# Seven block products in place of eight in six places of a two-layer macaron trunk

## The chip, the core and the metric

The kernel runs on one core of a Trainium2 chip. The metric is the device time of one execution in microseconds, given as the median over runs. Its engines are named as in the profile: PE is TensorE (matmuls), PEld its weight loads, DVE is VectorE, ACT is ScalarE, POOL is GpSimd, SP is SyncE (which here issues the DMAs).

## The reference

The input is x with 256 rows of 1024, and the model has two layers. Each layer is a macaron: a feed-forward with weight one half, a mixer, and a second such feed-forward, each behind an RMSNorm. The mixer of layer 0 is a convolution module, that of layer 1 a latent attention. A last RMSNorm ends the trunk. The change touches the feed-forwards alone:

```python
def swiglu_ffn(h, w1, w3, w2):
    return (jax.nn.silu(h @ w1) * (h @ w3)) @ w2
...
    h = h + FFN_RES_WEIGHT * swiglu_ffn(rmsnorm(h, ffn_norm1[i]), ffn1_w1[i], ffn1_w3[i], ffn1_w2[i])
```

w1 and w3 are 1024 x 2816, w2 is 2816 x 1024, and everything is float32. There are four feed-forwards, called FFN 0 to FFN 3 here: FFN 0 and 1 lie around the convolution module, FFN 2 and 3 around the attention.

## The kernel before

**Numbers.** Every float32 operand is held as two parts, a high part in TensorE's rounded float32 and a low part, the difference. A product is three matmuls into one PSUM bank (`mm3`, L274): high by low, high by high, low by high.

**Weights.** All weights come as blocks of 128 x 2048 float32, 1 MB each, in the one order in which they are used (the list `blocks` in `trunk`, L85). `load` (L164) fetches a block on SP's queue into one of three raw buffers (`RAW_BUFS`); ScalarE casts it to the high part in two pieces of 128 x 1024 (L190), and VectorE subtracts for the low part in two pieces (L191). There are five pairs of high and low buffers (`W_BUFS`), so the cast of a block waits until the block five places earlier has been read by TensorE. `weights` (L216) hands out the next block and loads ahead of it.

**A feed-forward** (`ffn_in`, L705). The first product goes in five chunks of 512 columns of w1 and w3: four blocks, 96 matmuls and four PSUM banks a chunk. A sixth, half chunk (`both`) takes two blocks. After a chunk, for each of the two halves of 128 rows (`tb`), ScalarE takes the Silu (L805), VectorE multiplies (L806), and `turn` transposes the result: VectorE transposes within 32 x 32 squares (L352), four DMAs write it to DRAM (L356) and one reads it back (L360), ScalarE casts the high part Gh (L714) and VectorE subtracts for the low part Gl (L715). `first_chunk` (L717) is the order of chunk 0 where the rows come in late. The second product (`Rows`, L626) has 11 blocks of w2 of two k tiles each; `block` (L640) issues the 24 matmuls of a block into four banks (two halves of rows by two halves of columns), and `finish` (L647) does the last blocks, the addition to h and the start of the next norm.

**PSUM.** Tag A has four banks and serves the chunks and the second product's four sums in turn, tag B three, tag C one.

**What sets the order.** The program is written in the order above, and a list scheduler puts each engine's instructions in order by its own timeline and by what is due; `urgent` (L196) gives an operation precedence, `order` adds an order between two instructions without a wait. An engine works through its own instructions strictly in that order.

Of the kernel before, what the change touches and what calls it, by code (L numbers as in the profile page):

```python
# [11 lines left out]
F32 = mybir.dt.float32  # L12
F32R = mybir.dt.float32r
# [3 lines left out]
ALU = mybir.AluOpType  # L17
AX = mybir.AxisListType

P = 128  # L20
D = 1024
S = 256
NT = S // P
KT = D // P
# [60 lines left out]
def trunk(ctx: ExitStack, tc: tile.TileContext, x, xt, first, pos, invf, gfin, wdw,  # L85
# [14 lines left out]
    def uid(s):  # L100
        n_uid[0] += 1
        return f"{s}_{n_uid[0]}"
# [4 lines left out]
    def bank(tag, name):  # L107
        return ps.tile([P, 512], F32, tag=tag, name=uid(name), bufs=BANKS[tag])

    blocks = []
    conv_block = {}
    for i in range(2):
        for w13, w2 in ((f1w13, f1w2), (f2w13, f2w2)):

            for cc_ in range(5):
# [3 lines left out]
            blocks += [w2[i, a_] for a_ in range(NF // 2)]  # L121
# [36 lines left out]
    def raw_to(last):  # L158
        while len(loaded) + len(raws) < last:
            src = blocks[len(loaded) + len(raws)]  # L160
            raw = rawp.tile([P, HB], F32, tag="raw", name=uid("raw"))
            raws[len(loaded) + len(raws)] = raw, nc.sync.dma_start(raw[:, :src.shape[-1]], src)

    def load(src, pieces=1):  # L164
        if isinstance(src, tuple):
            raw = rawp.tile([P, HB], F32, tag="raw", name=uid("raw"))
            nc.sync.dma_start(raw, src[1])
            return raw
        n = src.shape[-1]
        there = len(loaded) in raws  # L170
        raw = raws.pop(len(loaded))[0] if there else rawp.tile([P, HB], F32, tag="raw", name=uid("raw"))
        hi = wp.tile([P, HB], F32R, tag="hi", name=uid("hi"))
        lo = wp.tile([P, HB], F32R, tag="lo", name=uid("lo"))
        if there:
            pass
        elif len(loaded) < 7:

            for i in range(pieces if len(loaded) < 4 else 1):
                c = slice(i * n // pieces, (i + 1) * n // pieces) if len(loaded) < 4 else slice(n)
                fetch(raw[:, c], src[:, c])  # L180
        else:
            dma = nc.sync.dma_start(raw[:, :n], src)
            if turns:

                order(dma, turns[-1].ins)
        for i in range(pieces):
            c = slice(i * n // pieces, (i + 1) * n // pieces)

            low = nc.gpsimd if len(loaded) == conv_block[-4] else nc.vector
            casts[len(loaded), i] = (nc.scalar.copy(hi[:, c], raw[:, c]),  # L190
                                     low.tensor_sub(lo[:, c], raw[:, c], hi[:, c].bitcast(F32)))  # L191
# [79 lines left out]

    keep_warm(WARM)

    def mm3(o, ah, al, bh, bl, start, stop, after=()):  # L274

        mm = nc.tensor.matmul(o, ah, bl, start=start, stop=False)  # L276
        for a in after:
            order(mm, a.ins)
        nc.tensor.matmul(o, ah, bh, start=False, stop=False)  # L279
        return nc.tensor.matmul(o, al, bh, start=False, stop=stop)  # L280

    def some(o, kinds, ah, al, bh, bl, start, stop):

# [342 lines left out]
    class Rows:  # L626
        def __init__(self, zh, zl, nk, last=False):
            self.zh, self.zl, self.nk, self.last = zh, zl, nk, last
            self.o = {(tb, d): bank("A", "o") for tb in range(NT) for d in range(2)}

        def mm(self, part, i, tb, d, o, f0, f1, o0=0, o1=512, after=(), after_last=()):
            hi, lo = part
            for j in range(2):
                f = 2 * i + j
                c = slice(j * D + d * 512 + o0, j * D + d * 512 + o1)
                mm = mm3(o, self.zh[:, f, tbs(tb)], self.zl[:, f, tbs(tb)], hi[:, c], lo[:, c], f == f0,
                         f == f1 - 1, [*after, *after_last] if j else after)
            return mm

        def block(self, i):  # L640
# [57 lines left out]
            return nxt  # L698


    def ffn(X, make_next, beside=lambda: None, apart=False):
        with tc.tile_pool(name=uid("ffn"), bufs=1) as act:
            return ffn_in(act, X, make_next, beside, apart)

    def ffn_in(act, X, make_next, beside, apart):  # L705
# [40 lines left out]
        for c in range(6):  # L746
# [4 lines left out]
            u = {}  # L751
            if c == 0 and X.pool:
                first_chunk(X, u)
            for m in range(0 if u else 1 if both else 2):
                parts = weights(KT // kn, c > 0 or m > 0)
                before = None
# [49 lines left out]
                nc.vector.tensor_mul(s[:, :w], s[:, :w], u[0, tb][:, w:] if both else u[1, tb])  # L806
                turn(c, tb, w, s)
        o = Rows(Gh, Gl, NF, make_next is Final)
        for i in range(NF // 2 - (3 if apart else 2)):
            o.block(i)  # L810
            beside()
        return o.finish(X.rh, make_next, act, apart)
# [743 lines left out]
def _layout(x, positions, ffn_norm1, ffn1_w1, ffn1_w3, ffn1_w2, mix_norm, ffn_norm2,  # L1556
# [18 lines left out]
    def rows(w):  # L1575

        k, n = w.shape
        return c(w.reshape(k // (2 * P), 2, P, n).transpose(0, 2, 1, 3)).reshape(k // (2 * P), P, 2 * n)

    def halves(w):  # L1580

        k, n = w.shape
        return c(w.reshape(2, k // (2 * P), P, n).transpose(0, 2, 1, 3)).reshape(2, P, -1)
# [11 lines left out]
    for k in range(KT):  # L1595
# [22 lines left out]
        "f1w2": np.stack([rows(ffn1_w2[i]) for i in range(2)]),  # L1618
        "f2w13": np.stack([up(ffn2_w1[i], ffn2_w3[i]) for i in range(2)]),
        "f2w2": np.stack([rows(ffn2_w2[i]) for i in range(2)]),  # L1620
        "cw1": np.concatenate(cw1),
        "cw2": rows(conv_w_pw2[0]),
        "wa": np.concatenate([waq, wak]),
# [26 lines left out]
```

## Time and profile before

| | |
|---|---|
| three runs | 917.29, 914.8 and 916.79 us, median 916.79 us |
| span of the profiled execution | 913.0 us |
| DMA over the span | 198.94 MB moved, 218 GB/s in the mean |
| DMA of raw blocks of w1 and w3, w2 (in_f2w) | 66 of 1024 KB, 5.0 us from issue to landing |
| the same for in_f1w | 62 of 1024 KB, 5.2 us |

The span is the time from the first to the last instruction that the profiler recorded in one execution; the runs are timed from outside and are some microseconds longer. A page of the profile gives the busy time of each engine and the chain of work that ended last, followed back from the end. A row of a group reads: line, engine, operation, what it writes and reads with shapes, how often, then the busy time in all with the mean of one in nanoseconds, then the idle time ahead of it and what ended most of that. A row of the timeline reads: start, duration, engine, line, operation, how often, and in brackets the idle time ahead of it. The operations of an engine overlap a little at their ends, so the distance between two starts is somewhat less than a duration.

### The profile page before, as it was taken

To read this page: it belongs to the slowest core of one execution; us is meant where nothing else is said; L and a number is where in the kernel's file an instruction comes from. 1 tells how busy PE (TensorE), PEld (TensorE's weight loads), DVE (VectorE), ACT (ScalarE), POOL (GpSimd) and SP (SyncE) were. 2 spreads that over 40 slices of the span, in tenths; PEclk is the share of its full clock that TensorE was granted. 3 is DMA by queue.
4 is the path that set the end of the run, shared out by engine and by line. 5 is a ranking of instruction groups with operands and counts; after the bars stand their busy time and mean duration, and the time that the engine had idled before them with its cause. 6 is when DMAs were issued, how large, how long until landed. Compare 5 with 4: busy or idle time off the path is not lost.

```text
span 913.0 us, 12107 instructions
## 1 busy us (share of the span) xinstructions
PE 905.5 (99%) x4305; PEld 761.7 (83%) x4305; DVE 596.1 (65%) x940; ACT 495.8 (54%) x845; POOL 129.2 (14%) x259
## 2 busy tenths in 40 slices
PE   9999999999999999999999999999999999999997
PEld 7888888898988888888888888888898888888886
DVE  6885764489997666664486665545768567566533
ACT  7654544388876544543375444433677565454432
POOL 1730000079951000000020000001400000000000
PEclk9999999999999999999999999999999999999999
DMA  9987776533237977775577677754635468767611
GB/s 336 323 286 262 265 265 221 193 139 139 94 105 239 319 242 260 248 243 212 186 281 253 247 246 238 230 212 133 219 139 185 143 238 311 246 218 278 226 47 47
DMA packets 71053, 198.94 MB, mean 218 GB/s; under 512 B 12368, under 2 KB 41936, under 8 KB 51664
## 3 DMA queue, kind: packets, MB, share of 16 engines
q1 hardware_dynamic: 70560, 197.47, 62.7%
q8 instruction: 34, 0.56, 0.2%
q10 hardware_dynamic: 432, 0.69, 0.2%
q14 instruction: 27, 0.22, 0.1%
HBM read 181.87 MB, written 16.25 MB: 217 GB/s over the span
## 4 chain that ended last, share of the span: by engine, by line
PE 99%; ACT 0%; POOL 0%; DVE 0%; issue 0%; ACTq 0%
PE u L280 17%; PE u L279 17%; PE u L276 17%; PE o L279 10%; PE o L276 10%; PE o L280 10%; PE u L844 3%; PE gate L844 3%; PE u L285 2%; PE o L1080 2%; PE tp L320 1%; PE pairs L887 1%; PE a L280 1%; PE a L276 1%; PE a L279 1%; PE nope L276 1%
## 5 line engine op out<-in xcount | busy, mean ns | idle before, releaser
L191 DVE TENSOR_TENSOR lo<-raw,hi 128x1024 fp32r<-128x1024 f32 (+1 forms) x292 | 344.6, 1219 | 164.1 <-ACT hi L190 157.8
L190 ACT CAST hi<-raw 128x1024 fp32r<-128x1024 f32 x294 | 292.6, 1045 | 222.4 <-PE o L280 76.9
L276 PE MATMUL u<-lo,Xh 128*128 128x512 f32 x672 | 261.7, 389 | 0.0
L280 PE MATMUL u<-hi,Xl 128*128 128x512 f32 x672 | 261.6, 389 | 0.0
L279 PE MATMUL u<-hi,Xh 128*128 128x512 f32 x672 | 261.5, 389 | 0.0
L276 PEld LDWEIGHTS u<-lo,Xh 128*128 128x128 f32 x672 | 126.1, 188 | 26.7 <-ACT Xh L471 0.3
L280 PEld LDWEIGHTS u<-hi,Xl 128*128 128x128 f32 x672 | 126.1, 188 | 26.4 <-DVE Xl L339 0.4
L279 PEld LDWEIGHTS u<-hi,Xh 128*128 128x128 f32 x672 | 126.1, 188 | 26.1
L279 PE MATMUL o<-hi,Gh 128*128 128x512 f32 (+1 forms) x356 | 137.7, 387 | 0.0
L280 PE MATMUL o<-hi,Gl 128*128 128x512 f32 (+1 forms) x356 | 137.7, 387 | 0.0
L276 PE MATMUL o<-lo,Gh 128*128 128x512 f32 (+1 forms) x356 | 137.1, 387 | 0.0
L311 POOL TENSOR_TENSOR ms<-ss 128x1 f32<-128x1 f32 x16 | 10.5, 661 | 580.0 <-ACT junk L303 580.0
L276 PEld LDWEIGHTS o<-lo,Gh 128*128 128x128 f32 x356 | 66.9, 188 | 13.7
L280 PEld LDWEIGHTS o<-hi,Gl 128*128 128x128 f32 x356 | 66.8, 188 | 13.6
L279 PEld LDWEIGHTS o<-hi,Gh 128*128 128x128 f32 x356 | 66.9, 188 | 13.5
L714 ACT CAST Gh<-gb 128x512 fp32r<-128x512 f32 (+1 forms) x48 | 28.0, 583 | 79.6 <-DMA gb<-gd 79.6
L715 DVE TENSOR_TENSOR Gl<-gb,Gh 128x512 fp32r<-128x512 f32 (+1 forms) x48 | 31.3, 652 | 58.8 <-ACT Gh L714 58.8
L933 DVE SCALAR_TENSOR_TENSOR acc<-V,dw,acc 128x128 f32<-128x128 f32 (+1 forms) x174 | 53.9, 392 | 0.0
L954 ACT ACTIVATE prod<-V,dw 128x128 f32<-128x128 f32 (+1 forms) x128 | 45.6, 415 | 1.8 <-POOL Y L955 1.0
L806 DVE TENSOR_TENSOR s<-s,u 128x512 f32<-128x512 f32 (+1 forms) x48 | 30.4, 634 | 5.7 <-PE u L280 5.5
L665 DVE SCALAR_TENSOR_TENSOR h<-o,rh,h 128x512 f32<-128x512 f32 (+1 forms) x18 | 12.9, 719 | 32.5 <-PE o L280 32.5
L805 ACT ACTIVATE s<-u,R 128x512 f32<-128x512 f32 (+1 forms) x48 | 31.1, 647 | 4.7 <-PE u L280 3.7
(225 smaller groups left out, 904.5 us busy)
## 6 DMA issues: line engine op xcount, KB each, us to landing
raw<-in_f2w SPq DMA_DIRECT2D x66, 1024.0 KB, 5.0
raw<-in_f1w SPq DMA_DIRECT2D x62, 1024.0 KB, 5.2
raw<-in_cw SPq DMA_DIRECT2D x12, 1024.0 KB, 4.8
gd<-gt SPq DMA_DIRECT2D x160, 64.0 KB, 3.4
gb<-gd SPq DMA_DIRECT2D x40, 256.0 KB, 4.6
raw<-in_wo SPq DMA_DIRECT2D x4, 1024.0 KB, 4.8
hd<-rows SPq DMA_DIRECT2D x56, 64.0 KB, 2.3
rows<-hd SPq DMA_DIRECT2D x14, 256.0 KB, 2.7
```

What stands on the lines that cost most here:

```text
L190: casts[len(loaded), i] = (nc.scalar.copy(hi[:, c], raw[:, c]), low.tensor_sub(lo[:, c], raw[:, c], hi[:, c].bitcast(F32)))
L191: low.tensor_sub(lo[:, c], raw[:, c], hi[:, c].bitcast(F32)))
L276: mm = nc.tensor.matmul(o, ah, bl, start=start, stop=False)
L279: nc.tensor.matmul(o, ah, bh, start=False, stop=False)
L280: return nc.tensor.matmul(o, al, bh, start=False, stop=stop)
L714: nc.scalar.copy(gh, bv)
L715: nc.vector.tensor_sub(Gl[:, f, tbs(tb)].rearrange("p t (i q) -> p t i q", q=32), bv, gh.bitcast(F32))
L805: nc.scalar.activation(s[:, :w], u[0, tb][:, :w], AF.Silu, scale=X.r[tb])
L806: nc.vector.tensor_mul(s[:, :w], s[:, :w], u[0, tb][:, w:] if both else u[1, tb])
L844: mm = nc.tensor.matmul(u[:, t], w[:, c], X.x[:, k, t], start=(k == 0), stop=(k == KT - 1))
L933: dve_last.append(nc.vector.scalar_tensor_tensor(out if j == j1 - 1 else y, v, w, y, op0=ALU.mult, op1=ALU.add))
L954: prods_last.append(nc.scalar.activation(p, v, AF.Copy, scale=w))
```

## The change

A product of two matrices cut into 2 x 2 blocks takes eight products of blocks. Strassen's method (here in Winograd's form) takes seven, whose operands are sums and differences of the blocks. In FFN 1, 2 and 3 it is used twice: for chunk 3 of the first product (2 x 2 blocks of the rows: two halves of k by two halves of rows; of the weights: two halves of k by w1 and w3), and for the first eight k tiles of the second product, the first four blocks of w2. That makes six places, each called a seven below. The host lays out the first eight k tiles of w2 so that a fetched block of 128 x 2048 is one of the 2 x 2 blocks.

- `load_seven` fetches the four blocks as before, one DMA each. It forms the operands of the weights with four VectorE subtractions of 128 x 2048 in the raw buffers, and makes high and low parts of seven operands instead of four.
- `forms_of` makes the four operands of the rows that are sums or differences: a GpSimd addition of 128 x 2048 (high and low part back to one number), four GpSimd additions or subtractions of 128 x 512, and for each of these a ScalarE cast and a VectorE subtraction. For the first product it is called ahead of chunk 2's products; for the second product it reads the turned results of chunks 0 and 1.
- `seven_products` issues seven products of four k tiles each, 84 matmuls in place of 96. Partial sums go from bank to bank: c21 is copied from c11 (ScalarE), `kept` is a copy of c22 (ScalarE), c12 is c21 + kept (VectorE) and c22 is c21 + kept (VectorE) at a later state of c21, and TensorE goes on adding into them.
- There are four raw buffers in place of three, and the builder is given a smaller scratch area for dynamic DMAs.

FFN 0, the convolution module and the attention are not edited. In all, PE has 72 instructions fewer (matmuls), DVE 96 more, ACT 72 more, POOL 30 more, and SP as many as before.

```diff
-RAW_BUFS = 3
+RAW_BUFS = 4
...
+SEVEN_UP = {1: (3,), 2: (3,), 3: (3,)}
+SEVEN_DOWN = (1, 2, 3)
...
+    def seven(four):
+
+        group = {}
+        return [("seven", j, four, group) for j in range(7)]
...
+                if cc_ in SEVEN_UP.get(n_ffn, ()):
+                    four = [w13[i, m, 2 * cc_ + a_] for a_ in range(2) for m in range(2)]
+                    blocks += seven(four)
+                    continue
...
+            if n_ffn in SEVEN_DOWN:
+                blocks += seven([w2[i, a_] for a_ in range(4)])
...
+    def load_seven(j, four, b, pieces):
+        hi = wp.tile([P, HB], F32R, tag="hi", name=uid("hi"))
+        lo = wp.tile([P, HB], F32R, tag="lo", name=uid("lo"))
+        n = len(loaded)
+        if j == 0:
+            b[11], b[12] = fetched(four[0]), fetched(four[1])
+        elif j == 1:
+            b[22] = fetched(four[3])
+        elif j == 2:
+            b[21] = fetched(four[2])
+        sub = nc.vector.tensor_sub
+        if j == 1:
+            sub(b[11], b[12], b[11])
+            sub(b[12], b[22], b[12])
+        elif j == 2:
+            sub(b[11], b[22], b[11])
+        elif j == 6:
+            sub(b[11], b[21], b[11])
+        raw = b[(11, 11, 11, 21, 12, 22, 11)[j]]
+        for i in range(pieces):
+            c = slice(i * HB // pieces, (i + 1) * HB // pieces)
+            casts[n, i] = nc.scalar.copy(hi[:, c], raw[:, c]), sub(lo[:, c], raw[:, c], hi[:, c].bitcast(F32))
+        return hi, lo
...
+    def forms_of(xh, xl, sh, sl):
+
+
+        sh, sl = (z.rearrange("p k t -> p (k t)").rearrange("p (n k t) -> p n k t", n=4, t=P) for z in (sh, sl))
+        x = rows4.rearrange("p n t -> p (n t)").rearrange("p (k t) -> p k t", t=S)
+        add = nc.gpsimd.tensor_tensor
+        add(x, xh.bitcast(F32), xl.bitcast(F32), op=ALU.add)
+        x11, x12, x21, x22 = (x[:, 4 * a:4 * a + 4, tbs(tb)] for tb in range(2) for a in range(2))
+        for n, out, left, right, op in ((0, x22, x21, x22, ALU.add), (2, x21, x11, x21, ALU.subtract),
+                                        (1, x11, x22, x11, ALU.subtract), (3, x12, x12, x11, ALU.subtract)):
+            add(out, left, right, op=op)
+            nc.scalar.copy(sh[:, n], out)
+            nc.vector.tensor_sub(sl[:, n], out, sh[:, n].bitcast(F32))
+        return [(sh[:, n], sl[:, n]) for n in range(4)]
...
+        def product(a, b, fresh):
+            (hi, lo), = weights()
+            for k in range(4):
+                c = slice(k * 512, k * 512 + 512)
+                mm3(b, a[0][:, k], a[1][:, k], hi[:, c], lo[:, c], fresh and k == 0, k == 3, (), True)
+
+        c11, c21, c12, c22 = banks[0, 0], banks[1, 0], banks[0, 1], banks[1, 1]
+        product(rows(0, 0), c11, True)
+        urgent(nc.scalar.copy)(c21, c11)
+        product(forms[0], c22, True)
+        kept = tmp.tile([P, 512], F32, tag="s", name=uid("p5"))
+        urgent(nc.scalar.copy)(kept, c22)
+        product(forms[1], c21, False)
+        urgent(nc.vector.tensor_add)(c12, c21, kept)
+        product(rows(1, 0), c11, False)
+        product(forms[2], c21, False)
+        urgent(nc.vector.tensor_add)(c22, c21, kept)
+        product(forms[3], c12, False)
+        product(rows(1, 1), c21, False)
...
+            if seven_up and c == min(seven_up) - 1:
+                forms = forms_of(X.xh, X.xl, Gh[:, 14:], Gl[:, 14:])
+            if c in seven_up:
+                for key in ((0, 0), (0, 1), (1, 0), (1, 1)):
+                    u[key] = bank("A", "u")
+                seven_products(X.xh, X.xl, forms, {(tb, m): b for (m, tb), b in u.items()})
+                beside()
...
+        if seven_down:
+            sums = (xp.tile([P, KT, S], F32R, tag=tag, name=uid("rows")) for tag in ("Xh", "Xl"))
+            o.seven(forms_of(Gh[:, :8], Gl[:, :8], *sums))
+        for i in range(4 if seven_down else 0, NF // 2 - (3 if apart else 2)):
...
-    nc = _bacc.Bacc("TRN2", target_bir_lowering=False, num_devices=1)
+    nc = _bacc.Bacc("TRN2", target_bir_lowering=False, num_devices=1, dynamic_dma_scratch_size=1024)
```

The other edits carry a flag through `mm3` that lets matmuls add into a bank that another engine wrote, hand `ffn` the number of its feed-forward, and lay out w2 on the host.

More of the change, by code (lines that the diff above doesn't have):

```diff
@@ L120, in trunk @@
             blocks += [w13[i, a_, 10] for a_ in range(2)]
-            blocks += [w2[i, a_] for a_ in range(NF // 2)]
+            if n_ffn in SEVEN_DOWN:
+                blocks += seven([w2[i, a_] for a_ in range(4)])
+            blocks += [w2[i, a_] for a_ in range(4 if n_ffn in SEVEN_DOWN else 0, NF // 2)]
             if w13 is f1w13:
@@ L160, in raw_to, with fetched @@
             src = blocks[len(loaded) + len(raws)]
+            assert not isinstance(src, tuple)
             raw = rawp.tile([P, HB], F32, tag="raw", name=uid("raw"))
             raws[len(loaded) + len(raws)] = raw, nc.sync.dma_start(raw[:, :src.shape[-1]], src)
+    def fetched(src):
+        raw = rawp.tile([P, HB], F32, tag="raw", name=uid("raw"))
+        dma = nc.sync.dma_start(raw, src)
+        if turns:
+            order(dma, turns[-1].ins)
+        return raw
+    def load_seven(j, four, b, pieces):
[21 more added lines that the diff above has]
+        return hi, lo
     def load(src, pieces=1):
+        if isinstance(src, tuple) and src[0] == "seven":
+            return load_seven(*src[1:], pieces)
         if isinstance(src, tuple):
@@ L1578, in rows, with rows_seven @@
         return c(w.reshape(k // (2 * P), 2, P, n).transpose(0, 2, 1, 3)).reshape(k // (2 * P), P, 2 * n)
+    def rows_seven(w):
+        first = w[:8 * P].reshape(2, 4, P, 2, 512).transpose(0, 3, 2, 1, 4).reshape(4, P, HB)
+        return np.concatenate([c(first), rows(w)[4:]])
     def halves(w):
```

31 lines of the change are left out of this document (21 added, 10 removed).

## The prediction

> **What bounds the kernel now.** I read the page's head first, then the chain that ended last, then what TensorE waited for.
>
> ```profile
> span 913.0 us, 12107 instructions
> ...
> PE 905.5 (99%) x4305; PEld 761.7 (83%) x4305; DVE 596.1 (65%) x940; ACT 495.8 (54%) x845; POOL 129.2 (14%) x259
> ...
> PE 99%; ACT 0%; POOL 0%; DVE 0%; issue 0%; ACTq 0%
> ```
>
> ```profile
> PE warm L268 <- DVE still L263: 1.0, 1, 1.0
> PE rb L990 <- POOL rc L986: 0.4, 1, 0.4
> ```
>
> TensorE is busy 99% of the span, the chain is PE from end to end, and its waits sum to 1.4 us. So a matmul that goes away is time, and so is every wait that comes in. The next question is how much room the other engines have where the sevens go. Here are FFN 1's chunks 2, 3 and 4, its half chunk, the first four blocks of its second product, and the tail.
>
> ```profile
> core 0: us, PE busy (x) PEld busy (x) DVE busy (x) ACT busy (x) POOL busy (x), PEclk, DMA share, GB/s
> 321.30:343.00 21.70, 21.70 (x98) 17.96 (x97) 14.87 (x17) 10.10 (x12) 0.00 (x0) 1.00 0.73 237
> 343.00:364.70 21.70, 21.70 (x98) 17.96 (x97) 13.37 (x15) 10.34 (x12) 0.00 (x0) 1.00 0.74 256
> 364.70:386.40 21.70, 21.70 (x97) 18.00 (x96) 13.32 (x14) 10.43 (x12) 0.00 (x0) 1.00 0.72 241
> 386.40:397.30 10.90, 10.90 (x49) 9.01 (x49) 7.38 (x9) 5.24 (x7) 0.00 (x0) 1.00 0.87 289
> 397.30:419.00 21.70, 21.70 (x97) 17.98 (x96) 11.64 (x13) 9.35 (x12) 0.00 (x0) 1.00 0.65 217
> 905.00:913.00 8.00, 1.94 (x17) 1.73 (x15) 3.27 (x9) 2.76 (x8) 0.51 (x2) 0.82 0.36 131
> ```
>
> A chunk is 96 matmuls in 21.70 us: 0.226 us each, 5.43 us for a block's 24, 2.71 us for the 12 of one product of a seven. VectorE has about 8 us free in a chunk, ScalarE 11, GpSimd is idle. VectorE is the engine to watch.
>
> **The change part by part.** *TensorE.* A seven issues 7 x 4 x 3 = 84 matmuls in place of 96. Six sevens remove 72: 72 x 0.226 = **-16.3 us**. Bound: all of it comes only if nothing is late.
>
> *VectorE.* The durations:
>
> ```profile
> L191 DVE TENSOR_TENSOR lo<-raw,hi 128x1024 fp32r<-128x1024 f32 x288 | 341.6, 1225 | 164.1 <-ACT hi L190 157.8 <-PE u L285 5.3
> L352 DVE STREAM_TRANSPOSE gt<-s 128x512 f32<-128x512 f32 x40 | 28.4, 710 | 1.1
> L715 DVE TENSOR_TENSOR Gl<-gb,Gh 128x512 fp32r<-128x512 f32 x40 | 27.9, 697 | 42.8 <-ACT Gh L714 42.7
> L806 DVE TENSOR_TENSOR s<-s,u 128x512 f32<-128x512 f32 x40 | 27.1, 678 | 5.7 <-PE u L280 5.5
> ```
>
> ```profile
> 360.57 2.36 DVE L191 TENSOR_TENSOR lo<-raw,hi 128x1024 fp32r<-128x1024 f32 x2 [2.80 <-ACT hi L190]
> 362.85 0.68 DVE L806 TENSOR_TENSOR s<-s,u 128x512 f32<-128x512 f32 x1
> 365.60 0.71 DVE L352 STREAM_TRANSPOSE gt<-s 128x512 f32<-128x512 f32 x1
> 366.24 2.32 DVE L191 TENSOR_TENSOR lo<-raw,hi 128x1024 fp32r<-128x1024 f32 x2
> 375.09 0.62 ACT L714 CAST Gh<-gb 128x512 fp32r<-128x512 f32 x1 [1.36 <-DMA gb<-gd]
> ```
>
> From one start to the next, a pair of 128x1024 subtractions takes 362.85 - 360.57 = 2.28 us, so 1.14 each, and a transpose 0.64. With a 128x512 subtraction at 0.61 (0.697 less the same 0.09 of overlap), 512 more columns cost 0.53, and a 128x2048 subtraction, which the trace does not have, is 1.14 + 2 x 0.53 = 2.2 us (bounds: 2.1 from a line through zero and the 128x512 less its fixed part; 2.45 as two isolated 128x1024). The Trainium skill's "VectorE: DVE Perf Modes" (TRN2 errata section) gives 2.29 us for it, an estimate that would add 0.4 us to a seven.
>
> Each seven adds 3 hi/lo pairs (6.9), 4 subtractions of weights (8.8), 4 lows of the forms (2.4) and two 128x512 adds (1.4): 19.5 us, against 8 us free in a chunk. It can be spread only as far as the five hi/lo slots let VectorE run ahead: the first operand of a seven gets its slot when the block five places earlier has been read, 4 x 5.43 = 21.7 us before the seven's first product; its cast takes 1.3, and VectorE starts at -20.4. The last thing that VectorE owes in this stretch is the add into c12, since product 4 overwrites the bank c21 that it reads. In VectorE's order the pairs of all seven operands stand ahead of it. Product 4 is due at 4 x 2.71 = +10.9. So there are **31.2 us**, and the queue needs:
>
> - first product's seven: 7 pairs 16.0, 4 subtractions 8.8, two Gl 1.2, two multiplies 1.4, two transposes 1.3, the add 0.7, and 1.3 of waiting for a cast that needs a product's slot: **30.7**. It just fits.
> - second product's seven: pairs and subtractions 24.8, four Gl 2.4 (chunk 4's and the half chunk's turns end here), multiplies 2.2 and transposes 2.1 of the full and the half chunk, four lows of the forms 2.4, the add 0.7, waits 0.7: **35.3**. It is 4.1 short. TensorE waits, 3 x 4.1 = **+12.3 us**.
>
> Bounds: with subtractions at 2.1 and waits at nothing the second falls to 34.2 (+9.0 for three); at 2.45 it is 36.3 and the first 31.7 (+15.3 and +1.5).
>
> *GpSimd.* Each seven's forms cost one 128x2048 add and four 128x512 adds there. The trace has neither; the nearest rows:
>
> ```profile
> L191 POOL TENSOR_TENSOR lo<-raw,hi 128x1024 fp32r<-128x1024 f32 x2 | 4.7, 2363 | 1.8 <-ACT hi L190 1.8
> L955 POOL TENSOR_TENSOR Y<-Y,prod 128x256 f32<-128x256 f32 x15 | 10.8, 719 | 0.0
> ```
>
> (2363 - 719) / 768 = 2.14 ns a column: 128x512 is 1.27, 128x2048 is 4.55, a set 4.55 + 4 x 1.27 = **9.6 us** (bounds 9.4, by the larger row's mean rate of 2.31 ns, and 9.6 itself: the smaller row's 2.81 ns would give 11.5, but has a fixed part in every 256 columns). GpSimd has the room. What matters is whether these adds hold up VectorE. Rows where both engines work on two inputs in SBUF:
>
> ```profile
> 21.02 0.19 POOL L311 TENSOR_TENSOR ms<-ss 128x1 f32<-128x1 f32 x1 [16.36 <-ACT junk L303]
> 271.43 3.66 DVE L191 TENSOR_TENSOR lo<-raw,hi 128x1024 fp32r<-128x1024 f32 x3
> 272.97 0.86 POOL L311 TENSOR_TENSOR ms<-ss 128x1 f32<-128x1 f32 x1 [8.33 <-ACT junk L303]
> 283.61 1.25 POOL L311 TENSOR_TENSOR ms<-ss 128x1 f32<-128x1 f32 x1 [7.51 <-ACT junk L303]
> 281.32 3.49 DVE L191 TENSOR_TENSOR lo<-raw,hi 128x1024 fp32r<-128x1024 f32 x3
> ```
>
> ```profile
> 1.55 0.32 POOL L1515 TENSOR_TENSOR dpair<-ident 128x64 f32<-128x64 f32 x1
> 30.31 12.56 POOL L1521 TENSOR_TENSOR rows<-dpair,wpair 128x192 f32<-128x192 f32 x16 [6.43 <-DMA wpair<-in_wpair]
> 41.17 1.54 DVE L191 TENSOR_TENSOR lo<-raw,hi 128x1024 fp32r<-128x1024 f32 x1
> ```
>
> An operation on one column takes GpSimd 0.19 us alone and 0.86 or 1.25 beside VectorE's subtractions, about one subtraction's 1.14 longer. The other way, beside the run of 0.79 us adds (12.56 / 16) that start at 30.31 a subtraction shows 1.54 in place of a mean 1.22: it is late by about one small add (0.32 alone). I read both as: whoever starts first keeps the other out until its instruction ends. The Trainium skill's "SBUF — State Buffer" (section "SBUF: two separate sides") says so, an exclusive lock for the whole instruction between a VectorE operation with two SBUF inputs and a GpSimd one; the rows agree in both directions, with small adds alone.
>
> Where the sets fall: the forms of the first product's seven read Xh, Xl, there from chunk 0 on, and go by in chunks 0 and 1, where VectorE has 6 to 8 us free in a chunk and three blocks in store: nothing. The forms of the second product's seven need the last Gl of chunk 1, which follows that chunk's end by a turn (366.24 to 375.09, 8.8 us here) and one subtraction; that is -21.7 + 8.8 + 2 = about -11, in the middle of the first product's full stretch. If each add holds VectorE for its length: 30.7 + 9.6, less 1.3 (the wait for the cast is covered) and 0.7 (the part beside transposes and waits) = 38.3, which is 7.1 short: 3 x 7.1 = **+21.3 us**. Bounds: nothing, if GpSimd gets in only where VectorE is free; 9.6 x 3 = 28.8 in full.
>
> *ScalarE and the queues.* Six sevens add 72 operations to ScalarE: 6 casts of 128x1024, four of 128x512 and two copies from PSUM a seven.
>
> ```profile
> L190 ACT CAST hi<-raw 128x1024 fp32r<-128x1024 f32 x290 | 289.9, 1050 | 222.3 <-PE o L280 76.9 <-issue 55.9 <-PE u L280 55.9
> L714 ACT CAST Gh<-gb 128x512 fp32r<-128x512 f32 x40 | 24.7, 618 | 55.3 <-DMA gb<-gd 55.2
> ```
>
> 6 x 1.05 + 4 x 0.62 + 2 x 0.65 = 10.1 us a seven; free are 31.2 less 10.3 x 31.2 / 21.7 = 16. It hides (if not, up to 4 us a seven, inside the upper bound). The DMAs are as many as before, each raw tile once, and SP issues nothing more. A raw tile is now held until two or three products are formed from it; the fourth raw buffer is what lets the next block's fetch start meanwhile; a page row puts a 1 MB fetch at 5 us and a block lasts 5.43, so I take nothing (bounds: nothing, 2 us a seven). The copies c21 and kept stand ahead of their products by one product (2.71) and take about 0.65: nothing; without that cover 0.65 each. The changed scratch size moves no instruction. The instruction order in the conv module, the attention and FFN 0 is nearly as it was: nothing.
>
> **Sum:** 913.0 - 16.3 + 12.3 + 21.3 = 930.3 us of span. The three runs of before have a median of 916.79, 3.8 above the profiled span, and nothing shows what lies around it; with 3.8 added, **934 us**. For scale: 0.3% of 916.79, about what a measurement of this kernel can tell from no change, is 2.8 us.
>
> **The rivals.**
>
> *A, the forecast.* VectorE falls behind in both sevens and GpSimd's adds make the first worse: 928 to 946 (ends: 913.0 - 16.3 + 3.8 = 900.5, and to it 9.0 + 18.3, six sevenths of 21.3, or 16.8 + 28.8). For it: 31.2 us against 38.3 and 35.3.
>
> *B, GpSimd's adds cost VectorE a part.* VectorE's late subtraction above lost 0.3, not 0.8, and a large add that waits for its turn may be put off into VectorE's waits. With a half to three quarters of the 9.6, the first product's queue is 30.7 + 4.8 (or 7.2) - 2.0 = 33.5 (or 35.9), which is 2.3 (or 4.7) short: C's 912.8 below + 3 x 2.3 (or 4.7) = 920 (or 927), with the bounds 918 to 928.
>
> *C, the other side: GpSimd costs VectorE nothing in the stretch.* Then the first product's seven fits (30.7 of 31.2) and only 12.3 come back: 913.0 - 16.3 + 12.3 + 3.8 = **912.8**, faster than before; 909 to 918 by the bounds. It stays on that side while GpSimd's adds cost TensorE under 4.0 us in the three together (16.3 - 12.3), 1.3 each. Against it: the rows of 0.86 and 1.25. For it: only the smallest operations show a delay.
>
> *D, VectorE keeps up in both.* The queue's order or a shorter turn gives 4 us more in the second product: 913.0 - 16.3 + 3.8 = **900.5**, 899 to 904. This is the change doing all that it says.
>
> *E, worse than a queue.* TensorE's waits of 4 to 8 us also bring the clock down. The last row of the windows is the only place where TensorE stands still, from 906.95 on, and its mean clock there is 0.82. Were the next 4 us after each of six waits at half speed, 6 x 2 = 12 more: 946 to 958. The Trainium skill's "TensorE: Matmul & The Clock Gate" (Part 1) has the clock halve after about 3.4 us of idling; by that estimate both waits, 4.1 and 7.1, would be long enough.
>
> **How the numbers follow.** A 0.48, B 0.17, C 0.20, D 0.09, E 0.06. The time is A's, 934 us; its own range is 928 to 946. The range over the cases leaves out D and E (0.15): **909 to 946**. Faster by over 0.3% (under 914.0): D 0.09 and 0.11 of C, **0.20**. Within (to 919.5): 0.08 of C and 0.02 of B, **0.10**. Slower: **0.70**.
>
> **What would show it.** The matmul count falls by 72; if not, the first step is wrong. The list of TensorE's waits should have entries for VectorE, at the matmuls of products 1 to 4 of each seven, about 12 us in the second product's and 21 in the first's. VectorE should show no idle time in chunk 2 of FFNs 1 to 3. The 128x2048 subtractions should show 2.2 us, and the subtractions beside GpSimd's adds several us. If these show 1.2 us and GpSimd's adds are long instead, C holds; if TensorE shows no waits, D; a granted clock below 1.00 in the sevens is E. The forecast is wrong as well if the fetches turn up as what TensorE or ScalarE wait for.

## The result and the profile after

The changed kernel takes 959.74 us (median of 4 runs, 958.29 to 960.61) against 916.21 of the kernel before in the same comparison: a ratio of 1.0478 (95% interval 1.0463 to 1.0494). It is slower by 43.5 us; the forecast was 934 us with a range of 909 to 946.

The page of the changed kernel, its head and the chain that ended last:

```profile
span 958.4 us, 12212 instructions
...
PE 902.6 (94%) x4233; PEld 754.3 (79%) x4233; DVE 750.2 (78%) x1036; ACT 546.6 (57%) x917; POOL 215.0 (22%) x289
...
PE 46%; DVE 27%; DMA 14%; issue 7%; ACT 3%; SPq 2%; DVEq 0%; ACTq 0%
```

PE has its 72 matmuls fewer, but the chain is no longer PE alone: VectorE holds 27% of it and transfers 14%. What PE waited for in the changed kernel (total us, times, longest):

```profile
PE u L327 <- DVE s L915: 20.7, 2, 11.9
PE u L327 <- issue: 13.3, 1, 13.3
PE o L327 <- DVE s L915: 8.4, 3, 3.9
PE o L327 <- DVE o L253: 5.5, 3, 2.8
...
PE u L327 <- DVE u L253: 0.5, 1, 0.5
```

`u` is the first product, `o` the second: 34.5 us in the three sevens of the first, 13.9 in the three of the second, 48.4 in all. Most of it is before product 1, whose bank (c22) is the one that chunk 2's (or the half chunk's) multiply, L915, still has to read; L253 is the add into c12 or c22. The row "issue" is FFN 2's: the profile names no releaser for it, but there the multiply L915 ends at 551.21 and the matmul starts at 551.31. Behind five of the ten waits of 0.4 us or more the clock falls. Two stretches of the first seven in FFN 1, the wait and the 10 us behind it (us, PE, PEld, DVE, ACT, POOL busy, granted clock, DMA share, GB/s):

```profile
346.50:355.30 8.80, 0.05 (x1) 0.00 (x0) 8.80 (x6) 3.21 (x4) 8.57 (x4) 0.77 0.00 0
355.30:365.60 10.30, 10.26 (x33) 8.17 (x34) 10.30 (x11) 4.06 (x5) 0.52 (x1) 0.70 0.72 236
```

33 matmuls in 10.3 us, where 0.226 us each would give 46. Over the kernel, matmul starts that lie about 0.43 us apart instead of 0.226 cost about 10 us. With 913.0 - 16.3 + 48.4 + 10 = 955.1 the span of 958.4 is accounted for but for 3.3 us.

Waits and slow matmuls can be read as one number: how late product 4 of a seven starts, the first product that needs the add into c12 to be done. It is due 4 x 2.71 = 10.85 us after product 0. Its start in the trace, less the start of product 0 and these 10.85 us (product 0 is taken to start 2.71 us before the wait ahead of product 1), is:

| product 4 late by, us | FFN 1 | FFN 2 | FFN 3 | sum |
|---|---|---|---|---|
| first product's seven | 11.8 | 15.6 | 14.1 | 41.6 |
| second product's seven | 5.2 | 5.6 | 7.1 | 17.9 |

913.0 - 16.3 + 41.6 + 17.9 = 956.2, 2.2 us from the span.

### The profile page after: what moved, and what is told of

Same layout as the page of the kernel before. It is cut to its first block, busy times and chain, and to the rows that moved or that the text cites. A ratio compares the mean times of both kernels' runs of the same rounds, so it can differ in the third digit from the quotient of the medians.

```text
span 958.4 us, 12212 instructions
## 1 busy us (share of the span) xinstructions
PE 902.6 (94%) x4233; PEld 754.3 (79%) x4233; DVE 750.2 (78%) x1036; ACT 546.6 (57%) x917; POOL 215.0 (22%) x289
## 4 chain that ended last, share of the span: by engine, by line
PE 46%; DVE 27%; DMA 14%; issue 7%; ACT 3%; SPq 2%; DVEq 0%; ACTq 0%
PE o L327 8%; PE o L331 8%; PE o L330 8%; DVE lo L210 7%; DVE lo L242 6%; DMA gb<-gd 4%; DMA raw<-in_f2w 4%; PE u L330 3%; PE u L327 3%; PE u L331 3%; DMA gd<-gt 3%; DVE acc L1045 2%; DVE raw L204 2%; PE u L956 2%; PE gate L956 2%
## 5 line engine op out<-in xcount | busy, mean ns | idle before, releaser
L242 DVE TENSOR_TENSOR lo<-raw,hi 128x1024 fp32r<-128x1024 f32 (+1 forms) x244 | 309.1, 1309 | 77.8 <-ACT hi L241 77.4
L241 ACT CAST hi<-raw 128x1024 fp32r<-128x1024 f32 (+1 forms) x246 | 244.2, 1044 | 130.0 <-PE o L331 54.3
L327 PE MATMUL u<-lo,Xh 128*128 128x512 f32 x612 | 238.4, 389 | 0.1
L330 PE MATMUL u<-hi,Xh 128*128 128x512 f32 x612 | 238.1, 389 | 0.0
L331 PE MATMUL u<-hi,Xl 128*128 128x512 f32 x612 | 237.7, 389 | 0.0
L330 PE MATMUL o<-hi,Gh 128*128 128x512 f32 (+1 forms) x296 | 114.3, 386 | 0.0
L331 PE MATMUL o<-hi,Gl 128*128 128x512 f32 (+1 forms) x296 | 114.1, 386 | 0.0
L210 DVE TENSOR_TENSOR lo<-raw,hi 128x1024 fp32r<-128x1024 f32 x84 | 108.9, 1331 | 5.8 <-ACT hi L210 5.8
L210 ACT CAST hi<-raw 128x1024 fp32r<-128x1024 f32 x84 | 83.1, 1046 | 51.0 <-DVE raw L204 41.2
L343 POOL TENSOR_TENSOR rows<-rows 128x512 f32<-128x512 f32 x24 | 55.0, 2290 | 1.9
L327 PE MATMUL u<-lo,Gh 128*128 128x512 f32 x48 | 22.1, 461 | 34.5 <-DVE s L915 20.7
```

What stands on the lines that cost most here:

```text
L210: casts[n, i] = nc.scalar.copy(hi[:, c], raw[:, c]), sub(lo[:, c], raw[:, c], hi[:, c].bitcast(F32))
L327: mm = nc.tensor.matmul(o, ah, bl, start=start, stop=False, skip_group_check=seeded)
L330: nc.tensor.matmul(o, ah, bh, start=False, stop=False, skip_group_check=seeded)
L331: return nc.tensor.matmul(o, al, bh, start=False, stop=stop, skip_group_check=seeded)
L343: add(out, left, right, op=op)
```

## The experiments

Theory 1: GpSimd's adds shut VectorE out while it fills the first product's sevens. Rival, theory 2: VectorE's queue is too long by itself. Theory 3: raw buffers are held too long and fetches come late.

**GpSimd's adds away, all else in place.** Short diff, for the second product's forms alone; the orders on PE, DVE and ACT stay as they are:

```diff
-        add = nc.gpsimd.tensor_tensor
+        add = nc.gpsimd.tensor_tensor if adds else lambda *_, **__: None
...
+            o.seven(forms_of(Gh[:, :8], Gl[:, :8], *sums, adds=False))
```

> The five GpSimd adds of the forms of the second product are left out in FFNs 1 to 3 (the casts and subtractions that follow them read plain rows instead, so the second product is not that of the reference); the orders of PE, DVE and ACT are those of the changed kernel. Theory 1 (these adds shut VectorE out while it fills the first product's seven): of the 34.5 us that TensorE waits in the three sevens of the first product at most 6 are left, and the half clock behind them goes; the second product's 13.9 us stay; 913 to 925 us. Theory 2 (VectorE's queue alone: chunk 2's multiply stands behind the subtractions of the weights): 20 us or more are left in the first product, 940 us or more. Theory 3 (raw buffers held too long, fetches late): no change, 955 to 960.

938.05 us (ratio 1.0253, 1.0238 to 1.0268): 21.7 less than the change. Its waits:

```profile
PE u L327 <- DVE s L916: 9.8, 3, 4.3
PE o L327 <- DVE s L916: 6.5, 3, 4.1
PE o L327 <- DVE o L253: 6.5, 3, 2.8
PE u L327 <- DVE u L253: 2.1, 2, 1.8
```

The first product's waits fall from 34.5 to 11.9 us; the second's stay (13.0). So the adds cost 22.6 us of waits, and theories 1 and 2 both hold a part: 11.9 us are left that theory 1 had put at 6 or less. How the adds cost it is seen in the changed kernel, FFN 2, on GpSimd:

```profile
532.96 5.42 POOL L339 TENSOR_TENSOR rows<-Gh,Gl 128x2048 f32<-128x2048 f32 x1 [38.76 <-DVE Gl L817]
538.46 10.00 POOL L343 TENSOR_TENSOR rows<-rows 128x512 f32<-128x512 f32 x4
```

and on VectorE beside it:

```profile
533.96 6.57 DVE L204 TENSOR_TENSOR raw<-raw,raw 128x2048 f32<-128x2048 f32 x1
541.70 5.65 DVE L210 TENSOR_TENSOR lo<-raw,hi 128x1024 fp32r<-128x1024 f32 x3 [1.17 <-ACT hi L210]
547.26 3.35 DVE L206 TENSOR_TENSOR raw<-raw,raw 128x2048 f32<-128x2048 f32 x1
550.54 0.67 DVE L915 TENSOR_TENSOR s<-s,u 128x512 f32<-128x512 f32 x1
```

GpSimd's add of 128x2048 starts at 532.96; VectorE's subtraction, next in line at 533.96, shows 6.57 us in place of 2.29. It ends at 540.53, 2.2 us after the add has ended at 538.38: it ran only then. After that the two engines take turns: the three subtractions show 1.9 each instead of 1.17. The bank's multiply comes last of all, at 550.54. Without the adds the same operations (FFN 2 again, of the kernel without them) are:

```profile
508.25 0.68 DVE L916 TENSOR_TENSOR s<-s,u 128x512 f32<-128x512 f32 x1
508.96 0.71 DVE L446 STREAM_TRANSPOSE gt<-s 128x512 f32<-128x512 f32 x1
...
519.25 0.69 DVE L818 TENSOR_TENSOR Gl<-gb,Gh 128x512 fp32r<-128x512 f32 x1 [3.69 <-ACT Gh L817]
519.86 2.29 DVE L202 TENSOR_TENSOR raw<-raw,raw 128x2048 f32<-128x2048 f32 x1
...
525.05 2.29 DVE L204 TENSOR_TENSOR raw<-raw,raw 128x2048 f32<-128x2048 f32 x1
528.52 3.50 DVE L210 TENSOR_TENSOR lo<-raw,hi 128x1024 fp32r<-128x1024 f32 x3 [1.17 <-ACT hi L210]
531.93 2.28 DVE L206 TENSOR_TENSOR raw<-raw,raw 128x2048 f32<-128x2048 f32 x1
534.13 0.68 DVE L916 TENSOR_TENSOR s<-s,u 128x512 f32<-128x512 f32 x1
...
544.46 0.69 DVE L253 TENSOR_TENSOR u<-u,p 128x512 f32<-128x512 f32 x1
```

The subtractions L204, L210 (three) and L206 take 6.57 + 5.65 + 3.35 = 15.6 us beside the adds and 2.29 + 3.50 + 2.28 = 8.1 without them: 7.5 us for one set. There are two more things to see. Chunk 1's multiplies and transposes (508.25 on) stand in the stretch, which my count left out. And VectorE stands still for 3.69 us, full queue behind it, since the subtraction for chunk 1's Gl is next in its order and waits for that turn to come back from DRAM.

Here product 4 is late by 3.4, 6.4 and 7.1 us in the first product's sevens, 16.9 in all against 41.6 with the adds: 24.7 us. The run gained 21.7. Two half-clock stretches of its second product (granted clock 0.50 from 415.70 to 419.10 and from 603.40 to 606.80), some 1.7 us of loss each, lie behind product 4; in the changed kernel all of them lie ahead of it.

**The price of the adds.** Two edits of GpSimd's adds in the changed kernel, and one to VectorE:

```diff
+        x = rows4.rearrange("p n t -> p (n t)").rearrange("p (b k t) -> p b k t", b=NT, t=P)   # e_forms_packed
...
+            for k in (slice(0, 2), slice(2, 4)):                                                # e_adds_256
+                add(out[:, k], left[:, k], right[:, k], op=op)
...
+        add = nc.vector.tensor_tensor                                                           # e_forms_dve
```

> The sums of high and low part are laid out half of rows by half of rows, so that each 128x512 add of GpSimd reads and writes 512 consecutive columns instead of four runs of 128. It prices GpSimd's adds. If the runs of 128 made the 128x512 add 2.2 us instead of the 1.27 estimated, it is now 1.2 to 1.4 and a set about 10 us. Theory 1: the first product's waits fall by about the 4 us per set, from 34.5 to 20 to 25; 940 to 948 us. Theories 2 and 3: within 3 us of 959.7. If the add stays at 2.2, the layout is not its cause and nothing moves.

959.19 us (1.0489, 1.0473 to 1.0504): no change, and the 128x512 add keeps its 2.29 us, so the layout does not set it.

> Each 128x512 add of the forms on GpSimd as two of 128x256. It prices them. If an add of 256 columns costs the 0.72 us that the kernel before showed, a set's small adds take 8 x 0.72 = 5.8 us in place of 8.7, the first product's waits fall by 2 to 3 us a seven, and the time is 948 to 955. If two take as long as one of 512 (1.1 each), it stays within 2 us of 959.7.

954.41 us (1.0426, 1.0404 to 1.0448), inside the first expectation. The line of that add in this kernel (ns: least, median, most):

```profile
L344 POOL TENSOR_TENSOR rows<-rows x48: 716/1716/2772, 293.7 to 832.1; 128x256 f32<-128x256 f32 x48
```

The least, 716, is the 719 of the kernel before; the median is 1.0 us more, about one VectorE subtraction of 1.14. So the 2.2 us that most of the 128x512 adds show (2.29 in the mean) is probably not their own price either, but the 1.27 estimated plus a turn of VectorE's; no run shows a 128x512 add under 2.1 us.

> All adds of the forms on VectorE in place of GpSimd. A set is 2.2 + 4 x 0.6 = 4.7 us more for VectorE, against 14 to 16 us during which GpSimd held it. Theory 1: first product 30.7 - 1.3 + 4.7 = 34.1, about 3 short, 9 us of waits in place of 34.5; 925 to 938 us. Theory 2 (VectorE's queue is the cause, GpSimd's adds are not): more work in the same queue, 962 us or more.

939.54 us (1.0253, 1.0213 to 1.0292): 20 us better with more work on VectorE (waits 14.0 us in the first product), 1.5 above the range of theory 1 and far from theory 2's.

**Each kind of seven alone.** `SEVEN_DOWN = ()` and `SEVEN_UP = {}`.

> The sevens of the first product alone (36 matmuls fewer), so no GpSimd add falls into the full stretch. Theory 1: waits of 0 to 5 us in all: 916.2 - 8.1 + 1 to 6 = 909 to 914 us, at or below the kernel before. Theory 2: 6 to 9 us a seven remain and the clock falls: 930 to 942 us. Theory 3: as theory 2, with the wait put down to fetches.

928.31 us (1.0149, 1.0134 to 1.0164), a miss for theory 1 and 1.7 under theory 2's range: 15.1 us of waits and about 5 of slow matmuls are left with no GpSimd add of the second product's forms in the stretch.

> The sevens of the second product alone (36 matmuls fewer). The forms' set now falls into chunk 2 with no seven's operands beside it. Theory 1 (VectorE's queue ahead of the second product is short of time by itself): 4 to 5 us of waits a seven and some half clock, as in the whole: 915 - 8.1 + 14 + 4 + 1 = 924 to 928 us; with the sevens of the first product alone (+13.5) the two add up to about 25, and the 20 us more that both together cost are GpSimd's adds. Theory 2 (both sevens cost by following one another): no waits, 908 to 910.

928.74 us (1.0151, 1.0135 to 1.0166), 0.7 above the range of theory 1 and with the waits that it names, 13.3 us for VectorE. Alone they cost 13.5 and 13.6 us over the kernel before; together 43.5. The 16 us more fit the adds, which run in the first product's stretch only when both are there; taking the adds out gained 21.7, so the parts do not simply add up. Each kind of seven loses more than its 8.1 us by itself, and the next runs ask why.

**Order, amount, or standing still.** All on the kernel with the first product's sevens alone.

```diff
+            order(sub(b[11], b[21], b[11]), muls[-1].ins)     # e_first_mul_early: and the pairs of operands 3 to 6
...
-            sub(b[11], b[12], b[11])                          # e_first_no_subs: all four left out
```

> On the kernel with the first product's sevens alone: on VectorE the multiplies of chunk 2, which free the bank of product 1, come ahead of the subtraction for product 6 and of the pairs of operands 3 to 6. Theory Q (VectorE's whole queue up to the add into c12 is too long; the bank is only where it shows first): the 13.2 us of waits for the multiply fall by half or more, and come back at product 4 as waits for that add; 926 to 929 us, against 928.3. Theory O (the order alone is the fault): the waits go and do not come back, 912 to 918 us.

935.95 us (1.0227, 1.0212 to 1.0243), slower by 7.6 than without the edit. Its waits:

```profile
PE u L330 <- DVE u L256: 13.6, 3, 4.7
PE u L330 <- DVE s L918: 4.6, 2, 2.6
```

The bank comes early and the wait comes back, larger, at product 4 for the add into c12 (1.9 before, 13.6 now). Theory O falls; theory Q has the direction, not the size.

> The kernel with the first product's sevens alone, with the four VectorE subtractions of weights of a seven left out (the operands are then plain blocks, so chunk 3 is not that of the reference). VectorE has 9.1 us a seven less to do. Theory Q (VectorE's queue up to the add into c12 is 4 to 6 us too long): the 15.1 us of waits fall under 2 and the granted clock stays at 1.00: 907 to 911 us. If the waits came from the order, the turn's transfers or late fetches, 6 us or more stay: 916 or more.

913.69 us (0.9985, 0.9974 to 0.9996). That is between the two expectations. With 9.1 us less work a seven, 5.3 us of waits remain in the profiled run (916.43 us, the longest of ten); theory Q expected under 2. The median run is still 6.7 us above 915.14 - 8.1 = 907.0, so the amount counts, but it is not all.

> The kernel with the first product's sevens alone, with the split of chunk 1's turn into Gh and Gl put behind the seven's seven operands. Theory T: VectorE's 3.7 us of standing still and the 1.3 of the two subtractions leave the stretch; the 15.1 us of waits fall to 3 to 6, the half clock mostly goes: 913 to 919 us against 928.3. Rival (only the work counts, not the standing still): 13 us or more of waits, 925 or more.

```diff
+            if c + 2 in seven_up:
+                later.append(split)      # Gh and Gl of chunk 1, ordered behind the casts of the seven's last operand
```

The waits for VectorE of the kernel with the first product's sevens alone:

```profile
PE u L327 <- DVE s L915: 13.2, 3, 5.7
PE u L327 <- DVE u L253: 1.9, 1, 1.9
```

and with the split behind the operands:

```profile
PE u L327 <- DVE s L928: 7.5, 3, 3.4
PE u L327 <- DVE u L253: 0.7, 1, 0.7
```

921.4 us (1.0059, 1.0036 to 1.0081), 6.9 better: 15.1 us of waits become 8.2. No work is removed, but two subtractions of a seven (1.3 us) leave the stretch along with the standing still. The three sevens tell the two apart. Ahead of chunk 1's split VectorE had stood still for 0, 4.3 and 2.0 us in FFN 1, 2 and 3. Product 4 was late by 4.3, 7.9 and 8.5 us and is now late by 4.4, 2.5 and 6.5: nothing is gained where VectorE had not stood still, and most where it had longest. So theory T's mechanism holds. It expected 3 to 6 us of waits; what the rest comes from is not separated (one more subtraction, 1.1 us, now stands ahead of the multiply that frees the bank). The edit also gives the tile that the turn is read back into two more buffers; they are not the gain, since without them every read-back was issued 2.9 us or more after its buffer had come free.

**Sevens where the turns are over.** In the second product the plain blocks of k tiles 0 to 7 go first and the seven takes tiles 8 to 15, in four other banks; the plain sums are added to h behind it.

```diff
+            forms = forms_of(Gh[:, 8:16], Gl[:, 8:16], *sums)
+            for i in ahead:
+                o.block(i, 2 * ahead[-1] + 2)
+            o.seven(forms, X.rh)
```

> Sevens in the second product alone, on k tiles 8 to 15, begun after the first four plain blocks of w2 (five in FFN 3) in banks of their own; the plain blocks' sums are added to h by VectorE behind the seven. VectorE's turns are over by then, so its queue ahead of the add into c12 is 16.0 + 9.1 + 0.7 and about 2 of rest, 28 us of 31.2. Theory Q: waits under 2 us in all, no half clock, 36 matmuls fewer: 907 to 911 us, faster than the kernel before. If a seven costs waits wherever it stands: 920 or more.

928.09 us (1.0144, 1.0129 to 1.0159), a miss: 8.8 us of waits for the add into c12, 1.8 for multiplies and 3.3 at the start of norms. (The seven's sums in this kernel, in banks of tags B and C, are not the reference's; the next has the banks exchanged.)

> As the kernel with late sevens in the second product alone, with the PSUM banks exchanged: the plain blocks ahead sum up in the three banks of tag B and the one of tag C, the seven in tag A. It is the base of the next one. The same order of work, so the same 925 to 931 us, with about 3 us of waits a seven for the add into c12.

924.34 us (1.0093, 1.0077 to 1.0109), with 9.1 us of the same waits.

> Late sevens with the splits of the last turns into Gh and Gl (chunk 4 and half chunk; half chunk alone in FFN 3) put behind the seven's operands on ScalarE and VectorE, and two more buffers for what the turn reads back. Theory T (VectorE and ScalarE work in order, and stand still with the seven's operands behind a split that waits for the turn's transfers, 3 to 5 us a seven): the idle time before Gl goes, the waits for the add into c12 fall from 9 us to under 2, the half clock goes: 909 to 915 us, against 926 to 930 of the same without it. Rival (the seven's 28 us of VectorE work are too long for the run-ahead of five slots whatever stands ahead of them): 922 or more.

914.88 us (0.9997, 0.9986 to 1.0009), at the top of theory T's range and 9.5 us under the kernel that differs in where the split stands and in the two more buffers (without them a read-back found its buffer free for 3.2 us or more). The waits for the add fell from 9.1 to 2.9 us, all in FFN 3 (the profiled run was 921.08 us, the longest of ten, so its other waits are not read).

> The late sevens with the split of chunk 4's turn behind the seven's operands in FFN 3 too (four plain blocks ahead there as well). Theory T: the 2.9 us of waits of FFN 3's seven and the half clock behind them go as they did in FFN 1 and 2: 909 to 913 us, against 914.9. If FFN 3's wait has another cause, it stays at 914 to 916.

913.35 us (0.9979, 0.9970 to 0.9988): no wait is left at any seven. Theory T holds.

> The same in FFN 2 and 3 alone. In FFN 1 the seven's 2.7 us were outweighed by a wait of 2.6 us and slow matmuls at the start of the next norm, in FFN 2 by 1.4 us of wait. Theory T: 909.5 to 913 us, equal to or 2 us below the version with three.

912.22 us (0.9965, 0.9951 to 0.9979), faster than the changed kernel and 0.35% faster than the kernel before. The head of its page and all its waits but the first warm-up:

```profile
span 910.8 us, 12142 instructions
...
PE 900.7 (99%) x4281; PEld 757.2 (83%) x4281; DVE 653.7 (72%) x980; ACT 513.1 (56%) x869; POOL 155.3 (17%) x269
```

```profile
PE a L332 <- ACT Xh L570: 1.7, 1, 1.7
...
PE u L332 <- ACT Xh L570: 0.9, 2, 0.5
```

24 matmuls fewer are worth 5.4 us; 2.6 of them go into waits at the start of norms, and 2.2 are seen in the span.

**The clock and the buffers.**

> 84 small matmuls on zeros, some 9 us, stand between product 0 and product 1 of each of the first product's sevens, in the time in which TensorE waited for 8.8 to 13.3 us, so that it is not idle there for long. Theory A (the half clock after a wait comes from the wait and adds to the loss): the granted clock stays at 1.00 there, the 7.6 us of slow matmuls go, 951 to 955 us. Theory B (the slow matmuls are cover: product 4 waits for VectorE's add into c12 anyway, which comes at +10 us after product 1 whatever the clock): the clock stays up, but new waits for that add come in before product 4, and the time falls by 2 us at most: 957 to 960. Theory C (the half clock has another cause): clock as before.

980.2 us (1.0705, 1.0684 to 1.0725): inconclusive. The small matmuls had no order behind product 0, so a good part ran ahead of it and made the rest later, and 6.5 to 12.5 us of waits stayed.

> The kernel with the first product's sevens alone, and 34 small matmuls on zeros (3.6 us) ordered behind the last matmul of product 0, in the time in which TensorE waits 2.1, 5.4 and 5.7 us for product 1's bank. Theory A (half clock comes from the idle time and adds to the loss): the second and third waits shrink to about 2 us and the clock stays at 1.00 behind them; the first seven loses 1.5 us; 923 to 926 us against 928.3. Theory B (the slow matmuls are covered by VectorE's late add into c12): clock up, but waits before product 4 come in: 927 to 930. Theory C (another cause of the half clock): clock as before.

```diff
+        last = product(rows(0, 0), c11, True)
+        urgent(keep_warm)(34, after=last)
```

933.61 us (1.0208, 1.0193 to 1.0223), above both expectations. The waits for product 1's bank fell from 13.2 to 2.1 us and no half clock is left behind them, so the fall follows the idle time; but the filling itself takes 11 us, the waits for c12's add grew from 1.9 to 4.5 us as theory B says, and chunk 4 now waits 5.0 us for ScalarE's Silu. Behind one of those, of 2.19 us, the clock falls (the matmul that waited, then the stretch behind it with the granted clock in the last column but two):

```profile
366.14 0.79 PE L327 MATMUL u<-lo,Xh 128*128 128x512 f32 x1 [2.19 <-ACT s L916]
```

```profile
366.00:370.00 4.00, 3.86 (x10) 3.10 (x11) 4.00 (x5) 3.42 (x5) 0.00 (x0) 0.57 1.04 330
```

Theory B is also what product 4 shows: in FFN 1 it starts at 358.22 with the filling and at 358.74 without, both times 0.05 us after the add into c12 has ended.

The same reading says what the 10 us of slow matmuls cost in the changed kernel. The first product of FFN 2, from the end of the wait to product 4, and on VectorE and TensorE the add into c12 and the first matmul of product 4:

```profile
551.31:561.79 10.48, 10.48 (x36) 8.46 (x37) 10.48 (x12) 4.49 (x5) 0.00 (x0) 0.77 0.83 268
```

```profile
560.86 0.69 DVE L253 TENSOR_TENSOR u<-u,p 128x512 f32<-128x512 f32 x1
561.79 0.40 PE L327 MATMUL u<-lo,Gh 128*128 128x512 f32 x1
```

The 36 matmuls of products 1 to 3 take 10.48 us at a granted clock of 0.77 instead of 8.1, but VectorE is busy for all of the 10.48 us and its add ends at 561.55, 0.24 before product 4 starts. At full clock TensorE would have waited for that add. In the other five sevens it is the same: VectorE has no pause between the wait and the add, any half clock ends before product 4, and product 4 starts 0.05 to 0.4 us after the add. So nearly all of the 10 us stand where waits would have been.

> Four raw buffers and the smaller scratch area, no seven. It prices what the change moves in FFN 0 and elsewhere. The whole came 1.1 us late to the end of FFN 0. If that is from the fourth raw buffer: 915.5 to 916.5 us; if not, within 0.5 us of 915.1.

914.58 us (0.9994, 0.9985 to 1.0003): the fourth raw buffer and the scratch size cost nothing that can be measured. Theory 3 had fallen with the first run, which left buffers and fetches as they were and gained 21.7 us. Whether a fifth raw buffer would help was not tried.

## Why the prediction was wrong

**What held.** The saving (-16.3 us: PE's 4305 instructions became 4233). GpSimd's adds: 21.3 forecast; by the run without them 22.6 us of waits, or 24.7 us by how late product 4 starts. Their mechanism, read from operations of 0.19 us, held for those of 4.6. The raw buffers: nothing, as put. With the adds at this size, rivals B, C and D fall. The 128x2048 subtraction took 2.29 us; the 2.2 I worked out was low by 0.09, and here the Trainium skill's figure ("VectorE: DVE Perf Modes", TRN2 errata section) was the exact one.

**The step that failed:** "first product's seven ... **30.7**. It just fits." It did not: without GpSimd's adds 11.9 us of waits are left, and product 4 is 16.9 us late in the three sevens. The count was too low by two multiplies and two transposes (2.7 us, chunk 1's own, which stand behind the first operand's slot), and it counted work alone. VectorE also stood still for 3.7 us behind a split that waited for its turn. In FFN 2 of the kernel without the adds the stretch from 20.4 us ahead of product 0 to the end of the add into c12 is 37.6 us (507.6 to 545.15): 30.7 + 2.7 + 3.7 and 0.4 for the longer 128x2048 subtractions, where 31.2 were to be had. The prediction's own sign for this, no idle time of VectorE in chunk 2, failed too: the changed kernel has 3.0 us of it in FFN 2. And the wait shows at another place than the add into c12: 34.0 of the changed kernel's 34.5 us stand before product 1, whose bank waits for a multiply that comes behind the subtractions in the same queue. With that multiply put first it moved to product 4 and did not go, so the place was wrong and the queue was the cause. I had the time of a turn in hand (8.8 us) and used it to place GpSimd's adds, but not to ask what is queued behind the instruction that waits for it. In the kernel before, VectorE stands still ahead of its Gl as well (42.8 us over 40 of them), but there TensorE waits for nothing behind it.

**What only seems to have held:** the second product's queue, 4.1 us short a seven. Its waits, 13.9 us against 12.3, look near, but slow matmuls stand in place of more waits: product 4 is 17.9 us late. The count had 0.7 us of waits a seven; VectorE stood still for 1.8, 1.9 and 3.7 us there too, ahead of a Gl (changed kernel, at 393.33, 589.07 and 875.43).

**The clock** fell as rival E said, and its 12 us are near the 10 that the slow matmuls take. E added them to the waits, however, and the trace shows them in place of waits. So E's mechanism falls as well, and that the time came out near E's upper end is chance.

Together: 913.0 - 16.3 + 16.9 (first product's queue, forecast as nothing) + 24.7 (adds, 21.3) + 17.9 (second product's queue, 12.3) = 956.2, of 958.4 us of span. The range was too narrow since it let the first product's queue miss by 0.5 us a seven and no more.

## What to carry to other kernels

A count of work against time says whether a queue can keep up only if nothing in it waits: list, for the stretch, every instruction that waits for something slow (a round trip through DRAM) and what is due behind it, and move such instructions behind the urgent ones before judging the amount. Trading matmuls for elementwise work pays only in a stretch where the engine that takes it has that much time free, and a second engine's adds on the same memory are not free help. When a forecast has TensorE wait for some microseconds, expect slow matmuls behind the wait and ask what TensorE needs next: ahead of another late operand they cost next to nothing (the changed kernel), behind the last one they add to the loss (the kernel without the adds).

## What the runs showed of the hardware

GpSimd and VectorE alternate instruction by instruction when both are full: a 128x256 add shows 0.716 us at the least (0.719 in the mean of the kernel before) and 1.7 beside VectorE's subtractions, and a subtraction of 2.29 us shows 6.57 behind an add of 5.42. The Trainium skill's "SBUF — State Buffer" (section "SBUF: two separate sides") states the exclusive lock, and these traces agree for large operations too.

The half clock came also behind a wait of 2.19 us (0.57 in the row above), and behind one of 8.8 us it went on well after the work had come back: the stretch 355.30 to 365.60 still has 0.70. The Trainium skill's "TensorE: Matmul & The Clock Gate" (Part 1) puts it behind an idle window of about 3.4 us; here a shorter wait was enough. The length alone does not decide. Behind a wait of 2.82 us the clock is 0.50 in the kernel without the adds (415.70 to 419.10) and 1.00 in the changed kernel (619.30 to 623.30), where it is 0.57 behind one of 2.02 us (412.20 to 416.20).
